# An exponential that is traced one step later: order on ScalarE in the window attention of a fused encoder layer

## The chip, the cores and the metric

The kernel runs on one core of a Trainium2 chip. The metric is the device time of one execution in microseconds, the median of several runs. TensorE is written PE, VectorE DVE, ScalarE ACT, GpSimd POOL, SyncE SP; PEld is PE's weight loading. L420 is line 420 of the kernel before.

## What is computed

One encoder layer over 1024 tokens of width 1024, all in float32. A normed input goes through one projection, whose columns feed two attentions side by side; their outputs are normed, joined and projected back; a gated MLP with a short convolution and a last norm follow. The change touches the first attention:

```python
# group A: 8 query heads, 2 key/value heads of 64, window |i-j| <= 128, blocks of 128 queries
s = einsum('bqgrd,bkgd->bgrqk', q_i, k_i) * scale          # 128 queries x up to 384 keys
s = where(valid, s, -1e30)
m = maximum(max(s, axis=-1), sink)
p = exp(s - m)
denom = sum(p, axis=-1) + exp(sink - m)                     # the sink: one more column
o = einsum('bgrqk,bkgd->bgrqd', p, v_i) / denom
```

Group B, the second attention, is a neighbourhood attention over a 16 x 64 grid of tokens with a learned bias in place of the mask and without a sink.

## The kernel before

Products in float32 precision are made from a high and a low part of each operand: ACT rounds a tile to the format that PE multiplies fast (the high part), DVE subtracts that from the original (the low part), and PE runs three products, or two where one side needs no low part.

**The units.** The first attention has 16 units (2 key heads, 8 blocks of queries). A unit has four score steps (`q_step`, one per query head) and two or three transpose steps (`t_step`, one per block of keys; 44 in all).

- A score step runs two products into a PSUM bank `s` (L393, two such banks), then calls `softmax`.
- `softmax` has POOL copy the sink column beside the scores (L415, once per pair of heads), DVE add the mask and reduce to the negated maximum `nm` (L416), ACT take the exponential in place and sum it into `sm` (L420); with the second head of a pair DVE inverts both sums (L422) and POOL scales both heads' tiles (L424).
- A transpose step has PE transpose four 128 x 128 pieces of `p` into a bank `pt` (L456, two such banks); then `split_pt` has ACT copy the high part `ph` (L430) and DVE subtract to the low part `pl` (L431).
- The value step that belongs to it runs one event later: PE multiplies `ph` (L461) and `pl` (L462) by the values into a bank `o`. Behind the last one, `leave` has ACT copy half of `o` (`ot`, L474) and DVE add the halves (`mixa`, L478).

The second attention is built the same way with its own loops: scores through the same `softmax` without a sink, transposes at L531, value products at L542 and L543.

**The order of the work.** PE's order is the order in which the program is traced, written out by hand: per unit the list "t, q, v, q, t, q, v, t, q, v" for three blocks of keys, where q is a score step of a unit two ahead. Between these events a filler traces pieces of the input projection (L179 to L181), so many per event as the table `RATES` says; the projection's other work (`evacuate` L247, weights L171 and L172, rotations L261 to L263, splits L273 and L274) comes with it. The first eight score steps are traced ahead of the first transpose step.

ACT, DVE, POOL and SP are ordered by the framework's scheduler when the program is built: it takes the instruction that is ready by its own estimate and has the lowest rank, which is its place in the trace. `tc.high_priority(offset=n)` ranks what it encloses n instructions ahead of its place, and nested offsets add up. `softmax` uses 50, `split_pt` 100, evacuations 500. `behind(name)` forces a place in the queue: what it encloses is issued behind the marked instruction if it runs on the same engine; `mark["high"]` is the last traced `ph` copy. Once built, each queue's order is fixed.

The tiles `p` hold a pair of heads; five of them rotate, with some more borrowed from another pool. `nm` and `sm` have six buffers each.

Of the kernel before, what the change touches and what calls it, by code (L numbers as in the profile page):

```python
# [15 lines left out]
AF = mybir.ActivationFunctionType  # L16
ALU = mybir.AluOpType
# [41 lines left out]
def hybrid_layer(tc, xT, w_first, w_in, w_out, w_gate, w_up, w_down, small, sink, rpb, consts, rope, out):  # L59
    nc = tc.nc  # L60
    with ExitStack() as ctx:
# [19 lines left out]
        def bank(name, tag):  # L81
            return psum.tile([128, HALF], F32, name=name, tag=tag)
# [69 lines left out]
        mark = {}  # L152

        def behind(*names):

            stack = ExitStack()
            for n in names:
                stack.enter_context(tc.issue_after(mark[n].ins))
            return stack
# [224 lines left out]
        def near(b):  # L384
            return [c for c in (b - 1, b, b + 1) if 0 <= c < NB]
# [13 lines left out]
        def pair_tile(spare=False):  # L399
# [2 lines left out]
                return lpool.tile([128, 2, 386], F32, name="p", tag="mix", bufs=slots["mix"], padded_shape=[128, 2, 512])  # L402
            return apool.tile([128, 2, 386], F32, name="p", tag="p", bufs=5, padded_shape=[128, 2, 392])

        def softmax(st, j, ps, n, bias, nsink=None):

            w = lambda ap: ap.rearrange("p (s w) -> p s w", s=2)
            p = st["p"]
            with tc.high_priority(offset=50):
                nm = spool.tile([128, 1], F32, name="nm")  # L410
                if j == 0:
                    st["sm"], st["n"] = spool.tile([128, 2], F32, name="sm"), [n, n]
                sm, st["n"][j] = st["sm"], n
                if nsink is not None and j == 0:
                    nc.gpsimd.tensor_copy(p[:, 0:2, n:n + 1], nsink.rearrange("p (j o) -> p j o", o=1))  # L415
                nc.vector.tensor_tensor_reduce(  # L416
                    out=w(p[:, j, 0:n]), in0=ps[:, 0:n].rearrange("p (w s) -> p s w", s=2), in1=bias, scale=1.0, scalar=3e38 if nsink is None else nsink[:, j:j + 1],
                    op0=ALU.add, op1=ALU.min, accum_out=nm)
                e = n if nsink is None else n + 1
                nc.scalar.activation(p[:, j, 0:e], p[:, j, 0:e], AF.Exp, bias=nm, scale=-1.0, accum_out=sm[:, j:j + 1])  # L420
                if j == 1:
                    nc.vector.reciprocal(sm, sm)  # L422
                    for i, m in enumerate(st["n"]):
                        mark["scaled"] = nc.gpsimd.tensor_scalar(p[:, i, 0:m], p[:, i, 0:m], sm[:, i:i + 1], 1.0, op0=ALU.mult, op1=ALU.mult)  # L424

        def split_pt(ps, n):
            ph = apool.tile([128, HALF], F32R, name="ph", tag="ph")
            pl = apool.tile([128, HALF], F32R, name="pl", tag="pl")
            with tc.high_priority(offset=100):
                mark["high"] = nc.scalar.activation(ph[:, 0:n], ps[:, 0:n], AF.Copy)  # L430
                mark["rest"] = nc.vector.tensor_tensor(pl[:, 0:n], ps[:, 0:n], f32(ph[:, 0:n]), op=ALU.subtract)  # L431
            return ph, pl

        def unit_window(g, b):

            cs, n = near(b), 128 * len(near(b))
            ps4 = [None] * 4
            mask = w2(cst[:, K_MA + 128 * (cs[0] - b + 1):K_MA + 128 * (cs[-1] - b + 2)])
            st = {}

            def q_step(j):
                def go():
                    if j % 2 == 0:
                        st["p"] = pair_tile(True)
                    ps, _ = scores(qa[g, j // 2][j % 2], ka[g], b)
                    softmax(st, j % 2, ps, n, mask, nsink[:, 4 * g + j - j % 2:4 * g + j - j % 2 + 2])
                    ps4[j] = st["p"][:, j % 2, :]
                return go

            def t_step(i):  # L450
                def go():
                    if i == 0:
                        st["o"] = bank("o", "o")
                    pt = bank("pt", "pt")
                    for j in range(4):
                        nc.tensor.transpose(pt[:, j * 128:(j + 1) * 128], ps4[j][:, i * 128:(i + 1) * 128], ident)  # L456
                    ph, pl = split_pt(pt, HALF)

                    def v_step():
                        o, v = st["o"], va[g]  # L460
                        nc.tensor.matmul(o, v[:, cs[i], :], mv(ph[:, :]), start=i == 0, stop=False)  # L461
                        nc.tensor.matmul(o, v[:, cs[i], :], mv(pl[:, :]), start=False, stop=i == len(cs) - 1)  # L462
                        if i == len(cs) - 1:
                            leave()
                    return v_step
                return go

            def leave():
                ot = apool.tile([128, 2, 128], F32, name="ot", tag="ot", bufs=1, padded_shape=[128, 4, 128])
                o4 = pv(st["o"][:, :])  # L470
                halved = lambda ap: ap.rearrange("p (s w) -> p s w", s=2)
                for e in range(2):
                    me, other = slice(64 * e, 64 * e + 64), slice(64 - 64 * e, 128 - 64 * e)
                    nc.scalar.activation(ot[me].rearrange("p j (s w) -> p j s w", s=2), o4[other, e::2], AF.Copy)  # L474
                    for i in range(2):
                        if mix[2 * g + i] is None:
                            mix[2 * g + i] = big("mixa", "mix")
                        nc.vector.tensor_tensor(halved(mix[2 * g + i][me, b * 128:(b + 1) * 128]), o4[me, e + 2 * i], halved(ot[me, i, :]), op=ALU.add)  # L478

            return [q_step(j) for j in range(4)], [t_step(i) for i in range(len(cs))]  # L480
# [220 lines left out]
        nsink = cpool.tile([128, 8], F32, name="nsink")  # L701
# [172 lines left out]
        order = []  # L874
# [434 lines left out]
        order = []  # L1309
# [168 lines left out]
        def finish(h, v, cols=whole, split=False):  # L1478
            n = (cols.stop - cols.start) // 128
            wide = widen(v, "pt", n)  # L1480
            again = widen(v, "pt", n) if split else wide
            copy = half("wide")
            nc.scalar.activation(copy[:, cols], again[:, 0:128 * n], AF.Copy)  # L1483
            for d in (0, 1, 3, 2, 4, 6, 5, 7):
                x = at_res(d, h, cols)
                if d in APART:
                    nc.gpsimd.tensor_tensor(x, x, copy[:, cols], op=ALU.mult)  # L1487
                else:
                    nc.vector.scalar_tensor_tensor(x, x, col(C_NFIN + d), wide[:, 0:128 * n], op0=ALU.mult, op1=ALU.mult)
                (nc.scalar if split and d in (1, 4, 5) else nc.sync).dma_start(out[d, :, h * HALF + cols.start:h * HALF + cols.stop], x)  # L1490
# [24 lines left out]
        for i, (p, j, c) in enumerate(order):  # L1515
# [4 lines left out]
            f, n = PARTS[c]  # L1520
# [146 lines left out]
```

## Time and profile before

| what | value |
|---|---|
| median of 3 runs | 1018.97 us (1018.95 to 1019.7) |
| the profiled execution's own time | 1018.9 us |
| its span | 1017.1 us |
| granted PE clock, mean | 0.997 |
| exponentials on ACT (L420), 128 of them | 75.1 us, 587 ns each |
| scalings (L424), 128 of them | 75.4 us, 601 ns each |
| high parts (L430), 108 of them | 54.8 us, 508 ns each |
| low parts (L431), 108 of them | 63.6 us, 589 ns each |

The span is the time from the first to the last instruction that the profiler recorded. The first attention's score steps start at about 53 us and its last transposes end at about 181 us; the second attention runs from there to about 346 us. Rows of the timeline read: start in us, duration in us, engine, line, operation, output and inputs, their shapes, how many in a row; in brackets the idle time of the engine before it and what ended it. Rows of a view of waits read: engine, tile and line that waited, what it waited for, then us in total, times, longest. Ends of PE's rows are modelled, so the distance from one start to the next is the better measure there.

### The profile page before, as it was taken

What the parts mean: (1) busy time and instruction counts of PE and PEld (TensorE: products, weight loads), DVE (VectorE), ACT (ScalarE), POOL (GpSimd) and SP (SyncE); (2) the same over time, 40 slices, a digit from 0 to 9 for tenths busy, and PEclk for the clock granted to TensorE, in tenths of its full rate; (3) what the DMA queues carried; (4) which work ended last, traced back from release to release, by engine and by line L of the source; (5) the groups of instructions that cost most, each with busy time, mean ns of one, the idle gap of its engine ahead of it and who ended that gap; (6) DMA issues with size and microseconds to landing.
All of it is one profiled execution on the core that took longest, in us unless ns stands there. A gap on an engine that the chain in (4) does not pass through costs nothing.

```text
span 1017.1 us, 14843 instructions
## 1 busy us (share of the span) xinstructions
PE 1006.8 (99%) x5086; PEld 889.0 (87%) x5086; DVE 833.2 (82%) x1566; ACT 561.0 (55%) x1081; POOL 103.8 (10%) x188
## 2 busy tenths in 40 slices
PE   9999999999999999999999999999999999999996
PEld 8898888999899888888888888888888888888886
DVE  7889888768888899999987786786777678996765
ACT  8567786657687554555544443444443645544451
POOL 0223333222332100000000000000000000000002
PEclk9999999999999999999999999999999999999998
DMA  8223022333234456231552333323232699966644
GB/s 294 83 73 94 30 73 65 83 83 83 84 93 136 125 193 222 82 103 64 188 191 90 111 114 114 104 94 125 93 133 85 228 329 322 312 225 235 225 153 166
DMA packets 68220, 144.94 MB, mean 142 GB/s; under 512 B 8240, under 2 KB 18736, under 8 KB 68144
## 3 DMA queue, kind: packets, MB, share of 16 engines
q1 hardware_dynamic: 58208, 118.88, 36.4%
q10 hardware_dynamic: 9936, 25.11, 6.4%
q8 instruction: 40, 0.66, 0.3%
q14 instruction: 36, 0.29, 0.1%
HBM read 103.58 MB, written 28.57 MB: 130 GB/s over the span
## 4 chain that ended last, share of the span: by engine, by line
PE 88%; DVE 6%; ACT 2%; issue 2%; DMA 1%; SPq 0%; DVEq 0%; ACTq 0%
PE x L1026 7%; PE x L1027 7%; PE x L1028 7%; PE dn L1028 7%; PE dn L1027 7%; PE dn L1026 7%; PE pj L179 7%; PE pj L181 6%; PE pj L180 6%; PE y L1027 4%; PE y L1026 4%; PE y L1028 4%; PE s L393 3%; PE z L1026 2%; PE z L1027 2%; PE z L1028 2%
## 5 line engine op out<-in xcount | busy, mean ns | idle before, releaser
L1026 PE MATMUL x<-hg,whi 128*128 128x512 f32 x352 | 133.5, 379 | 0.0
L1027 PE MATMUL x<-hg,whi 128*128 128x512 f32 x352 | 133.4, 379 | 0.0
L1028 PE MATMUL x<-hg,wlo 128*128 128x512 f32 x352 | 133.4, 379 | 0.0
L1026 PE MATMUL dn<-xd,whi 128*128 128x512 f32 (+1 forms) x330 | 120.8, 366 | 0.0
L1028 PE MATMUL dn<-xd,wlo 128*128 128x512 f32 (+1 forms) x330 | 120.6, 365 | 0.0
L1027 PE MATMUL dn<-xd,whi 128*128 128x512 f32 (+1 forms) x330 | 120.5, 365 | 0.0
L420 ACT ACTIVATE p<-p,nm 128x385 f32<-128x385 f32 (+3 forms) x128 | 75.1, 587 | 62.3 <-DVE nm L416 58.0
L1000 ACT ACTIVATE whi<-ws 128x512 fp32r<-128x512 f32 (+1 forms) x100 | 60.7, 621 | 74.2 <-DVE ws L1136 14.7
L179 PE MATMUL pj<-xgh,whi 128*128 128x512 f32 x245 | 99.7, 407 | 0.1
L424 POOL TENSOR_SCALAR p<-p,sm 128x384 f32<-128x384 f32 (+1 forms) x128 | 75.4, 601 | 196.6 <-DVE sm L422 165.8
L180 PE MATMUL pj<-xgl,whi 128*128 128x512 f32 x245 | 93.1, 380 | 0.2
L181 PE MATMUL pj<-xgh,wlo 128*128 128x512 f32 x245 | 92.9, 379 | 0.0
L1000 ACT ACTIVATE whi<-raw 128x512 fp32r<-128x512 f32 (+1 forms) x102 | 60.9, 610 | 51.0 <-PE x L1027 17.3
L1001 DVE TENSOR_TENSOR wlo<-ws,whi 128x512 fp32r<-128x512 f32 (+1 forms) x100 | 66.5, 680 | 19.2 <-ACT whi L1000 18.8
L431 DVE TENSOR_TENSOR pl<-pt,ph 128x384 fp32r<-128x384 f32 (+2 forms) x108 | 63.6, 589 | 18.1 <-ACT ph L430 16.4
L1028 PEld LDWEIGHTS x<-hg,wlo 128*128 128x128 f32 x352 | 66.5, 189 | 9.5
L1026 PEld LDWEIGHTS x<-hg,whi 128*128 128x128 f32 x352 | 66.5, 189 | 9.4
L1027 PEld LDWEIGHTS x<-hg,whi 128*128 128x128 f32 x352 | 66.5, 189 | 9.4
L1487 POOL TENSOR_TENSOR h<-h,wide 128x256 f32<-128x256 f32 (+1 forms) x6 | 5.4, 914 | 669.4 <-ACT wide L1483 669.4
L1001 DVE TENSOR_TENSOR wlo<-raw,whi 128x512 fp32r<-128x512 f32 (+1 forms) x102 | 66.5, 668 | 6.7 <-ACT whi L1000 4.5
L1028 PEld LDWEIGHTS dn<-xd,wlo 128*128 128x128 f32 x330 | 62.5, 189 | 7.9 <-DVE wlo L1001 0.3
L1027 PEld LDWEIGHTS dn<-xd,whi 128*128 128x128 f32 x330 | 62.5, 189 | 7.7
(267 smaller groups left out, 2495.0 us busy)
## 6 DMA issues: line engine op xcount, KB each, us to landing
xd<-x SPq DMA_DIRECT2D x77, 256.0 KB, 5.0
raw<-in_w_down_dram SPq DMA_DIRECT2D x72, 256.0 KB, 4.6
raw<-in_w_gate_dram SPq DMA_DIRECT2D x22, 512.0 KB, 3.5
raw<-in_w_up_dram SPq DMA_DIRECT2D x22, 512.0 KB, 3.6
x<-c ACTq DMA_DIRECT2D x22, 512.0 KB, 2.8
raw<-in_w_in_dram SPq DMA_DIRECT2D x30, 256.0 KB, 2.8
raw<-in_w_down_dram SPq DMA_DIRECT2D x36, 192.0 KB, 4.4
x<-t ACTq DMA_DIRECT2D x11, 512.0 KB, 2.6
```

What stands on the lines that cost most here:

```text
L179: nc.tensor.matmul(ps, w[0], mv(x[0][:, tsl(h)]), start=first, stop=False)
L180: nc.tensor.matmul(ps, w[0], mv(x[1][:, tsl(h)]), start=False, stop=False)
L181: nc.tensor.matmul(ps, w[1], mv(x[0][:, tsl(h)]), start=False, stop=last)
L393: nc.tensor.matmul(ps[:, 0:n], qs, k[i][:, cs[0] * 128:cs[0] * 128 + n].rearrange("p (s w) -> p w s", s=2), start=i == 0, stop=i == 1)
L420: nc.scalar.activation(p[:, j, 0:e], p[:, j, 0:e], AF.Exp, bias=nm, scale=-1.0, accum_out=sm[:, j:j + 1])
L424: mark["scaled"] = nc.gpsimd.tensor_scalar(p[:, i, 0:m], p[:, i, 0:m], sm[:, i:i + 1], 1.0, op0=ALU.mult, op1=ALU.mult)
L431: mark["rest"] = nc.vector.tensor_tensor(pl[:, 0:n], ps[:, 0:n], f32(ph[:, 0:n]), op=ALU.subtract)
L1000: nc.scalar.activation(hi, src, AF.Copy)
L1001: nc.vector.tensor_tensor(lo, src, f32(hi[:, :, :]), op=ALU.subtract)
L1026: nc.tensor.matmul(ps, w[0], x[0], start=first and i == 0, stop=False, skip_group_check=True)
L1027: nc.tensor.matmul(ps, w[0], x[1], start=False, stop=False, skip_group_check=True)
L1028: nc.tensor.matmul(ps, w[1], x[0], start=False, stop=last and i == len(ws) - 1, skip_group_check=True)
```

## The change

The exponential of a score, and with the second head of a pair the reciprocal and the two scalings, are put into a function that is kept in a list and run later. The list is emptied at three places: at the start of the next `softmax`; in a transpose step of the first attention, right behind `split_pt`, there with the exponential forced behind that step's `ph` copy on ACT; and at once, at the end of `softmax`, if there is no sink (the second attention). Wherever it is emptied, what it traces is enclosed in a priority of 50 at that place. In the second attention that place is inside `softmax`'s own block of 50.

```diff
+        deferred = []
+
+        def exponentials(*order):
+            while deferred:
+                with tc.high_priority(offset=50):
+                    deferred.pop(0)(*order)
+
         def softmax(st, j, ps, n, bias, nsink=None):
 
+            exponentials()
             w = lambda ap: ap.rearrange("p (s w) -> p s w", s=2)
...
                 e = n if nsink is None else n + 1
-                nc.scalar.activation(p[:, j, 0:e], p[:, j, 0:e], AF.Exp, bias=nm, scale=-1.0, accum_out=sm[:, j:j + 1])
-                if j == 1:
-                    nc.vector.reciprocal(sm, sm)
-                    for i, m in enumerate(st["n"]):
-                        mark["scaled"] = nc.gpsimd.tensor_scalar(p[:, i, 0:m], p[:, i, 0:m], sm[:, i:i + 1], 1.0, op0=ALU.mult, op1=ALU.mult)
+                widths = list(st["n"])
+
+                def finish(*order):
+                    with behind(*order):
+                        nc.scalar.activation(p[:, j, 0:e], p[:, j, 0:e], AF.Exp, bias=nm, scale=-1.0, accum_out=sm[:, j:j + 1])
+                    if j == 1:
+                        nc.vector.reciprocal(sm, sm)
+                        for i, m in enumerate(widths):
+                            mark["scaled"] = nc.gpsimd.tensor_scalar(p[:, i, 0:m], p[:, i, 0:m], sm[:, i:i + 1], 1.0, op0=ALU.mult, op1=ALU.mult)
+
+                deferred.append(finish)
+                if nsink is None:
+                    exponentials()
...
                     ph, pl = split_pt(pt, HALF)
+                    exponentials("high")
 
                     def v_step():
```

## The prediction

> **What bounds the kernel now.** I read the page first, for the whole span.
>
> ```profile
> span 1017.1 us, 14843 instructions
> PE 1006.8 (99%) x5086; PEld 889.0 (87%) x5086; DVE 833.2 (82%) x1566; ACT 561.0 (55%) x1081; POOL 103.8 (10%) x188
> ```
>
> PE is the bound of the program: 1006.8 of 1017.1 us. The edit removes no work from PE, so it can win only time in which PE stands still for want of something that ACT delivers. The profiled execution took 1018.9 us, 1.8 more than its span; the median shown is 1018.97. I make the sum on the span and carry it over to the median unchanged.
>
> Next I compared, in the table by windows, the stretch of the first attention in which PE isn't solid with the one behind it.
>
> ```profile
> core 0: us, PE busy (x) PEld busy (x) DVE busy (x) ACT busy (x) POOL busy (x), PEclk, DMA share, GB/s
> 65.00:110.00 45.00, 44.03 (x251) 38.64 (x249) 39.90 (x120) 33.56 (x86) 17.08 (x38) 1.00 0.30 75
> 110.00:180.00 70.00, 70.00 (x399) 62.85 (x399) 58.70 (x172) 50.07 (x128) 22.39 (x48) 1.00 0.20 55
> ```
>
> By PE's own column 45.00 - 44.03 = 0.97 us are missing between 65 and 110, and none later. By the weight loads, a clean stretch is busy 62.85 / 70.00 = 0.898 of its time, and this one 38.64 / 45.00 = 0.859: the difference is 0.039 / 0.898 x 45 = 2.0 us. The clock is 1.00 in both rows, so it explains nothing. Which of the two is the ceiling of the gain? The gaps below add up to 1.8 us, so I take 2.0.
>
> The Trainium skill (Perfetto Trace Analysis, Identifying the Most-Contended Engine) says that matmul busy time is a poor measure of TensorE's headroom and that the share of weight loads is a better one. The trace agrees: 2.0 against 0.97. By the poorer column the most that this stretch could give would be 0.97 us, 1018.0.
>
> Then the waits of the weight loads from 65 to 340 us, both attentions, and ACT's groups from 65 to 110 us (last column: idle time of ACT just before them and who ended it).
>
> ```profile
> PEld o L462 <- DVE pl L431: 2.1, 4, 0.7
> PEld o L543 <- DVE pl L431: 1.0, 2, 0.7
> PEld s L393 <- DVE nm L416: 0.4, 2, 0.2
> ```
>
> ```profile
> L420 ACT ACTIVATE p<-p,nm 128x385 f32<-128x385 f32 (+1 forms) x25 | 15.0, 598 | 10.7 <-DVE nm L416 9.0 <-POOL p L424 1.2 <-DVE sm L422 0.5
> L430 ACT ACTIVATE ph<-pt 128x512 fp32r<-128x512 f32 x18 | 10.6, 587 | 0.4 <-PE pt L456 0.2
> ```
>
> PE waits in its value products (o, L462) for the low part pl, which DVE makes from ph, which ACT makes from the transposes. ACT isn't full (33.56 of 45): it idles 9.0 us in front of exponentials whose maximum nm isn't there, and almost never (0.4) in front of ph. So ph is late not for want of ACT time, but because it stands in the queue behind an exponential that waits for DVE.
>
> **The change part by part.** Per window unit four scores are traced, one step at a time between transposes. Their exponentials (ACT), the reciprocal (DVE) and the two scalings (POOL) used to be traced with the score; now they are traced at the next score (24 of 64) or right behind the next ph (40 of 64: every one of the first 40 chunks finds exactly one pending). No instruction is added or removed: 128 exponentials, 128 scalings, no DMA, nothing on SP. What changes is order, on three queues. I replay the stalls with the durations of the rows.
>
> Stall B, the largest: ACT, then PE, then DVE.
>
> ```profile
> 98.08 0.62 ACT L420 ACTIVATE p<-p,nm 128x385 f32<-128x385 f32 x1 [0.37 <-DVE nm L416]
> 98.61 0.19 ACT L420 ACTIVATION_READ_ACCUMULATOR p<-p,nm 128x1 f32 x1
> 99.28 0.62 ACT L420 ACTIVATE p<-p,nm 128x385 f32<-128x385 f32 x1 [0.49 <-DVE sm L422]
> 100.41 0.60 ACT L430 ACTIVATE ph<-pt 128x512 fp32r<-128x512 f32 x1
> ...
> 98.06 0.60 PE L456 MATMUL pt<-cst,p 128*128 128x128 f32 x4
> 101.22 0.38 PE L461 MATMUL o<-ph,v 128*128 128x512 f32 x1
> 102.03 0.48 PE L462 MATMUL o<-pl,v 128*128 128x512 f32 x1 [0.43 <-DVE pl L431]
> ...
> 99.18 0.46 DVE L478 TENSOR_TENSOR mixa<-o,ot 64x128 f32<-64x128 f32 x2
> 100.42 0.29 DVE L478 TENSOR_TENSOR mixa<-o,ot 64x128 f32<-64x128 f32 x1 [0.78 <-ACT ot L474]
> 101.29 0.69 DVE L431 TENSOR_TENSOR pl<-pt,ph 128x512 fp32r<-128x512 f32 x1
> ```
>
> The transposes end at 98.66 and ACT is free at 98.80, but ph starts at 100.41. Behind the edit ph starts at 98.8 and ends at 99.4; the exponential of 99.28 follows it at about 99.3, because ph fills the 0.49 us in which ACT was idle. The low part fits into DVE's 0.78 us of idling before 100.42 and is done at about 100.3, before 101.22. L461 to L462 took 0.81 us where an undisturbed pair takes 0.22 (106.98 to 107.20 in the rows for POOL below); the stalled matmul's row is 0.10 longer as well (0.48 against 0.38). Worth: 0.6 + 0.1 = 0.7 us.
>
> Stall A, the same pattern: ACT, then PE.
>
> ```profile
> 88.95 0.38 ACT L474 ACTIVATE ot<-o 64x256 f32<-64x256 f32 x1
> 89.62 0.62 ACT L420 ACTIVATE p<-p,nm 128x385 f32<-128x385 f32 x1 [0.30 <-DVE nm L416]
> 90.36 0.60 ACT L430 ACTIVATE ph<-pt 128x512 fp32r<-128x512 f32 x1
> ...
> 88.02 0.60 PE L456 MATMUL pt<-cst,p 128*128 128x128 f32 x4
> 91.27 0.38 PE L461 MATMUL o<-ph,v 128*128 128x512 f32 x1
> 91.79 0.48 PE L462 MATMUL o<-pl,v 128*128 128x512 f32 x1
> ```
>
> ph can start at 89.3 instead of 90.36, a microsecond earlier; the exponential slips from 89.62 to about 89.9. Worth: 0.52 - 0.22 + 0.1 = 0.4 us.
>
> Stall C is different: ACT, DVE, PE.
>
> ```profile
> 106.84 0.59 ACT L430 ACTIVATE ph<-pt 128x512 fp32r<-128x512 f32 x1
> ...
> 107.63 0.81 DVE L172 TENSOR_TENSOR wlo<-raw,whi 128x512 fp32r<-128x512 f32 x1
> 108.76 0.68 DVE L431 TENSOR_TENSOR pl<-pt,ph 128x512 fp32r<-128x512 f32 x1
> ...
> 108.72 0.38 PE L461 MATMUL o<-ph,v 128*128 128x512 f32 x1
> 109.50 0.48 PE L462 MATMUL o<-pl,v 128*128 128x512 f32 x1 [0.40 <-DVE pl L431]
> ```
>
> Here ph is done at 107.43 and pl starts at 108.76: DVE's own queue (weights, two score additions) is what is late, and no order on ACT mends that. I leave its 0.78 - 0.22 + 0.1 = 0.7 us standing.
>
> What the move costs. The exponential comes 0.05 to 0.3 us later in A and B, and one ph (0.60) later at most; reciprocal and scalings follow it. Cover: the scaled p are wanted late. POOL, then PE:
>
> ```profile
> 102.59 1.51 POOL L424 TENSOR_SCALAR p<-p,sm 128x384 f32<-128x384 f32 x2 [1.96 <-DVE sm L422]
> ...
> 106.98 0.38 PE L461 MATMUL o<-ph,v 128*128 128x512 f32 x1
> 107.20 0.38 PE L462 MATMUL o<-pl,v 128*128 128x512 f32 x1
> 107.41 0.27 PE L456 MATMUL pt<-cst,p 128*128 128x128 f32 x1
> ```
>
> The scalings end at 104.10 and the first transpose that reads them starts at 107.41: 3.3 us of cover, the shortest of the 16 units, so I cost the delay at nothing. Were the cover gone, each of 16 units would lose up to the 0.6 us. On POOL the copy of the sink column of the next pair may fall behind a later scaling; that delays an exponential, under the same cover. On DVE the reciprocal may block the queue while its exponential is late; that happened for 0.5 us in 65 to 110 (the exponential's row above names sm for that much), and nothing that I see makes it more.
>
> The second attention changes too, though it isn't named. Its exponentials are still emitted with the score, but from inside the block of priority 50 and with another 50 around them; nested offsets add, so exponential, reciprocal and scalings now rank 100 traced instructions ahead, level with ph and pl. Where both are ready, an exponential traced before a ph now goes first. The trace of before can't show what that does. Bounds, from the stretch 275 to 337 us (who waited for ph there, then ACT, then DVE):
>
> ```profile
>   DVE pl L431: 2.7, 8
> ...
> 333.62 0.49 ACT L430 ACTIVATE ph<-pt 128x384 fp32r<-128x384 f32 x1
> 334.01 0.60 ACT L420 ACTIVATE p<-p,nm 128x384 f32<-128x384 f32 x1
> ...
> 335.05 0.54 DVE L431 TENSOR_TENSOR pl<-pt,ph 128x384 fp32r<-128x384 f32 x1
> ```
>
> At most, at the 8 chunks where DVE waits for ph, each ph falls behind one exponential of 0.6 us: 8 x 0.6 = 4.8 us slower. At best the two waits of L543 go: 1.0 us faster. I take 0, by the nearest rows: flipping the pair at 333.62 would end ph at about 334.7, still before its pl starts at 335.05, and ACT mostly issues the earlier traced exponential first already.
>
> Sum: -0.7 (B) - 0.4 (A) + 0 (C) + 0 (cover) + 0 (second attention) = -1.1 us. Span 1017.1 to 1016.0, median 1018.97 to **1017.9**. Behind 110 us PE is solid, so what is won there stays won.
>
> **The rivals.**
>
> R1, it mends more than I count. An earlier ph pulls pl forward on DVE everywhere, C dissolves too and the whole 2.0 us return, with one of the two waits of L543 (0.5): 1018.97 - 2.5 = 1016.5; with both, 1016.0. For it: DVE has 45 - 39.90 = 5.1 us idle here. Against it: in C pl stood behind ready work of DVE, not behind ACT.
>
> R2, DVE takes over. It is busy 39.90 of 45. An earlier pl (0.69) goes ahead of the score additions, nm comes later, and PE waits for the score's bank instead (L393 already waits 0.4 us, two times). The 1.1 us come back as two to four waits of 0.3: 1019.0. The Trainium skill (the same section) says to go for the engine with the highest occupancy first; here that is DVE, ahead of ACT, and by that rule an order on ACT gives nothing, 1019.0. The trace bears it out only in part, since A and B show DVE idle or on work that can wait.
>
> R3, slower: the second attention. Its exponentials, now level with ph, go ahead of it between 275 and 337 us, where PE has little reserve. With three quarters of the upper bound, 3.6 us, against the 1.1 won: 1018.97 + 2.5 = 1021.5; at the full bound 1022.7. It decides from two such chunks on (1.2 us eat the gain). For it: PE waits 1.0 us for pl there already. Against it: the replayed pair, where the flip costs nothing.
>
> That the edit doesn't do what it says is not likely: the order behind ph is forced, not left to priorities.
>
> **How the numbers follow.** A measurement of this kernel tells about 0.2%, 2.04 us, from no change: the borders are 1016.93 and 1021.01. Forecast 1017.9: 0.32, its own range 1017.0 to 1018.6, of which 0.05 lies below the lower border. R1: 0.24, of which 0.21 below it. R2: 0.12, all between. R3: 0.32, from 1019.5 upwards, of which 0.28 lies above the upper border, since a reordered queue can cost more than the rows let me price. Faster 0.26, same 0.46, slower 0.28. The range for 8 in 10 takes in R1 with both waits gone and most of R3: 1015.9 to 1022.4.
>
> **What would show it.** Right: on ACT from 65 to 110 us ph follows its transposes within about 0.5 us and the 9.0 us of waiting for nm shrink; the gaps at A and B are gone; L462's wait falls from 2.1 to about 0.7; PEld in 65 to 110 rises towards 39.9. R2: L393's wait for nm grows to 1 us or more. R3: L543's wait grows above 2 us, and exponentials precede ph there. Wrong altogether: PE waits for POOL at the transposes (L456), or ACT's idle time stands in front of ph, with PE late in return.

## The result, and the profile after

| | before | after |
|---|---|---|
| median of 11 runs each, same chip | 1018.97 us (1018.2 to 1019.97) | 1016.21 us (1015.73 to 1017.16) |
| ratio | | 0.9972, 95% interval 0.9964 to 0.998 |
| profiled execution, own time | 1018.9 us | 1016.91 us |
| its span | 1017.1 us | 1015.1 us |

The kernel is 2.76 us faster; the forecast was 1.1. The profiled execution of the changed kernel was 0.7 us slower than its median, so the two traces differ by 2.0 us only, and that much can be followed in them.

In the changed kernel the score addition is L424 (was L416), the exponential L432 (L420), the reciprocal L434 (L422), the scalings L436 (L424), the high part L446 (L430), the low part L447 (L431); in the first attention the transposes are L472 (L456) and the value products L478 and L479 (L461 and L462), in the second L548, L559 and L560 (L531, L542 and L543). Kernels of the experiments are a few lines off these.

The page of the changed kernel; the last row is that of the chain that ended last, where PE had 88% before and DVE 6%:

```profile
span 1015.1 us, 14835 instructions
PE 1006.3 (99%) x5086; PEld 890.2 (88%) x5086; DVE 832.7 (82%) x1566; ACT 561.8 (55%) x1081; POOL 104.0 (10%) x188
...
PE 99%; DVE 1%; issue 0%; ACT 0%; DVEq 0%; POOL 0%; POOLq 0%
```

PE's work is the same 1006 us; what went is time in which it stood still. The table by windows, same columns as before:

```profile
65.00:110.00 45.00, 45.00 (x261) 40.20 (x260) 41.02 (x124) 34.61 (x88) 18.10 (x40) 1.00 0.31 77
110.00:180.00 70.00, 70.00 (x399) 62.95 (x399) 58.73 (x174) 50.99 (x131) 22.44 (x48) 1.00 0.20 54
```

Between 65 and 110 us the weight loads rise from 38.64 to 40.20 of 45 us, nearly the share of the clean stretch behind it (62.95 / 70 x 45 = 40.5). The waits of the weight loads from 65 to 340 us, then ACT's groups from 65 to 110 us:

```profile
PEld o L560 <- DVE pl L447: 0.5, 2, 0.3
PEld s L393 <- DVE nm L424: 0.3, 1, 0.3
PEld o L479 <- DVE pl L447: 0.3, 1, 0.3
```

```profile
L432 ACT ACTIVATE p<-p,nm 128x385 f32<-128x385 f32 (+1 forms) x26 | 15.4, 592 | 4.4 <-DVE nm L424 4.1 <-DVE sm L434 0.3
L446 ACT ACTIVATE ph<-pt 128x512 fp32r<-128x512 f32 x18 | 10.7, 595 | 5.7 <-PE pt L472 5.5
```

The wait for the low part in the first attention falls from 2.1 to 0.3 us, that in the second from 1.0 to 0.5. ACT's idle time in front of exponentials falls from 10.7 to 4.4 us and turns up in front of the high part (0.4 to 5.7), where it means that ACT stands ready before the transposes are done.

Where the gain sits is read off the starts of five rows of PE: the first transpose, the low-part products behind A, B and C, the last such product of the first and of the second attention. In the changed kernel, leaving out what lies between:

```profile
65.21 0.27 PE L472 MATMUL pt<-cst,p 128*128 128x128 f32 x1
...
91.64 0.38 PE L479 MATMUL o<-pl,v 128*128 128x512 f32 x1
...
101.18 0.38 PE L479 MATMUL o<-pl,v 128*128 128x512 f32 x1
...
108.26 0.42 PE L479 MATMUL o<-pl,v 128*128 128x512 f32 x1
...
184.21 0.38 PE L479 MATMUL o<-pl,v 128*128 128x512 f32 x1
...
345.31 0.28 PE L560 MATMUL o<-pl,v 128*128 128x256 f32 x1
```

In the kernel before the same starts were 91.79, 102.03 and 109.50 (in the rows of A, B and C above), and

```profile
64.86 0.27 PE L456 MATMUL pt<-cst,p 128*128 128x128 f32 x1
...
185.72 0.38 PE L462 MATMUL o<-pl,v 128*128 128x512 f32 x1
...
347.20 0.28 PE L543 MATMUL o<-pl,v 128*128 128x256 f32 x1
```

The distance from one start to the next, after minus before, is -0.50 (up to A), -0.70 (A to B), -0.39 (B to C), -0.27 (C to the end of the first attention) and -0.38 us (second attention), together -2.24; the trace of after starts its transposes 0.35 us later. That shift is there at 34 us already, ahead of the first score step, so it isn't the edit's.

### The profile page after: what moved, and what is told of

Read it like the earlier page. It is cut to its first block, busy times and chain, and to the rows that moved or that the text cites. A ratio compares the mean times of both kernels' runs of the same rounds, so it can differ in the third digit from the quotient of the medians.

```text
span 1015.1 us, 14835 instructions
## 1 busy us (share of the span) xinstructions
PE 1006.3 (99%) x5086; PEld 890.2 (88%) x5086; DVE 832.7 (82%) x1566; ACT 561.8 (55%) x1081; POOL 104.0 (10%) x188
## 4 chain that ended last, share of the span: by engine, by line
PE 99%; DVE 1%; issue 0%; ACT 0%; DVEq 0%; POOL 0%; POOLq 0%
PE pj L179 8%; PE pj L181 8%; PE pj L180 8%; PE x L1045 7%; PE x L1043 7%; PE x L1044 7%; PE dn L1045 7%; PE dn L1044 7%; PE dn L1043 7%; PE s L393 4%; PE y L1045 4%; PE y L1043 4%; PE y L1044 4%; PE pt L472 2%; PE z L1043 2%; PE z L1045 2%
## 5 line engine op out<-in xcount | busy, mean ns | idle before, releaser
L432 ACT ACTIVATE p<-p,nm 128x385 f32<-128x385 f32 (+3 forms) x128 | 75.1, 587 | 47.0 <-DVE nm L424 44.1
L436 POOL TENSOR_SCALAR p<-p,sm 128x384 f32<-128x384 f32 (+1 forms) x128 | 75.6, 603 | 196.0 <-DVE sm L434 179.9
L447 DVE TENSOR_TENSOR pl<-pt,ph 128x384 fp32r<-128x384 f32 (+2 forms) x108 | 63.3, 586 | 17.4 <-ACT ph L446 16.3
L446 ACT ACTIVATE ph<-pt 128x384 fp32r<-128x384 f32 (+2 forms) x108 | 55.3, 512 | 25.8 <-PE pt L472 14.4
```

## The experiments

This table gives the same five distances for every kernel, each minus that of the kernel before, in us from one profile each, beside the ratio of the medians to the kernel before on the same chip (95% interval). One profile tells a column to about 0.2 us, at times only to 0.5: in "exponential 100" the first attention's queues are those of the kernel before, and A came out 0.46 shorter all the same; "changed kernel" and "grid as before" have the same queues there, and C differs by 0.34.

| kernel | to A | B | C | rest of first | second attention | ratio |
|---|---|---|---|---|---|---|
| changed kernel | -0.50 | -0.70 | -0.39 | -0.27 | -0.38 | 0.9972 (0.9964 to 0.998) |
| grid as before | -0.49 | -0.70 | -0.73 | -0.31 | +0.07 | 0.9983 (0.9974 to 0.9992) |
| grid only | -0.09 | +0.01 | -0.01 | +0.03 | -0.72 | 0.9992 (0.9983 to 1.0001) |
| not forced | +0.04 | -0.04 | -0.01 | +0.02 | -0.67 | 0.9998 (0.9989 to 1.0006) |
| first 27 scores | -0.49 | -0.70 | +0.04 | -0.04 | -0.58 | 0.9982 (0.9974 to 0.9991) |
| from the 28th score | -0.05 | 0.00 | 0.00 | -0.21 | -0.74 | 0.9991 (0.9982 to 1.0) |
| low part first at C | -0.09 | +0.01 | -0.42 | -0.01 | -0.08 | 0.9996 (0.9987 to 1.0005) |
| one more late | +0.57 | -0.51 | -0.20 | -0.31 | -0.49 | 0.9991 (0.9982 to 1.0) |
| all behind the high part | -0.50 | -0.70 | -0.73 | -0.31 | -0.52 | 0.9975 (0.9965 to 0.9984) |
| inverse and scale 100 | -0.10 | +0.21 | -0.01 | 0.00 | -1.00 | 0.9991 (0.9982 to 1.0) |
| exponential 100 | -0.46 | +0.01 | -0.02 | 0.00 | +0.18 | 1.0001 (0.9993 to 1.001) |
| both deferred | -0.49 | -0.70 | -0.73 | -0.31 | +0.78 | 0.9983 (0.9975 to 0.9992) |
| both findings | -0.50 | -0.70 | -0.73 | -0.31 | -0.87 | 0.9972 (0.9962 to 0.9981) |

### Which half brings what

*Grid as before*: the changed kernel, with the second attention's exponentials, reciprocals and scalings at their old rank.

```diff
                 if nsink is None:
-                    exponentials()
+                    deferred.pop()()
```

> The changed kernel, but in the second attention the exponentials, reciprocals and scalings keep their old priority of 50. Theory (the gain is the first attention's: ph no longer stands behind exponentials that wait for nm): PE is solid from 65 to 110 us as in the changed kernel, weight loads there near 40.2 us of 45, and the median is 2.0 to 2.8 us below before. In the trace the second attention falls back by at most 0.4 us, since its start differs from before only by the shift. Rival (the second attention's priority 100 brings a good part): the median is at most 1.8 us below before, and between 275 and 337 us the waits of the value products for pl return to 1.0 us of weight-load waiting.

*Grid only*: the kernel before, with the second attention's three kinds of instructions at rank 100 and nothing deferred.

```diff
+                with tc.high_priority(offset=50 if nsink is None else 0):
                     nc.scalar.activation(p[:, j, 0:e], p[:, j, 0:e], AF.Exp, bias=nm, scale=-1.0, accum_out=sm[:, j:j + 1])
                     if j == 1:
...
```

> The kernel before with the one edit that its second attention's exponentials, reciprocals and scalings rank 100 instead of 50. Theory: the first attention is untouched, 2.1 us of weight-load waiting for pl and the three gaps stay, and the median moves by less than 0.5 us, to between 1018.4 and 1019.2. Rival (that priority is worth something): 0.5 to 1.0 us faster, with L543's waits halved. The prediction's third rival (it costs): 1.2 to 4.8 us slower.

Measured: 1017.22 against 1018.96 us (-1.74) and 1018.07 against 1018.96 (-0.89). The two add up to -2.63, beside -2.76 for the whole change, and the table shows each gain in its own columns alone. So the part that the change is named for brings some two thirds, and the rank of the second attention, which it isn't named for, a third. The interval of the second one ends at 1.0001; that it is a gain rests also on the second-attention column, which is -0.4 to -1.0 in all nine kernels that raise the reciprocals' rank, and -0.08 to +0.18 in the three that leave them where they were.

### The forced place

*Not forced*: the changed kernel without the order behind the high part; the exponentials are still traced there.

```diff
-                    exponentials("high")
+                    exponentials()
```

> The changed kernel without the forced place behind ph: exponentials are traced one step later, but only their rank orders them. Theory (the forced place is what does it, since the scheduler takes nm to be ready sooner than it is and puts the exponential first again): most phs stand behind a waiting exponential as before, ACT idles 7 us or more in front of exponentials between 65 and 110 us, at least two of the three gaps are back, and the median is 0 to 1 us below before. Rival (being traced later, and so ranked behind ph, is enough): as the changed kernel, 2 us or more below before.

Measured: 1018.78, ratio 0.9998. In the weight loads from 65 to 110 us everything is back:

```profile
PEld o L479 <- DVE pl L447: 2.1, 4, 0.7
```

Tracing the exponential later is worth nothing by itself in the first attention. The place in the queue is what counts, and the scheduler, left to its ranks, puts the exponential back in front. The second attention keeps its -0.67, which the interval of the ratio takes in.

### Stall C, which I had left standing

In the changed kernel DVE's queue at C is this:

```profile
106.73 0.81 DVE L172 TENSOR_TENSOR wlo<-raw,whi 128x512 fp32r<-128x512 f32 x1
107.46 0.68 DVE L447 TENSOR_TENSOR pl<-pt,ph 128x512 fp32r<-128x512 f32 x1
108.06 0.47 DVE L424 CUSTOM_DVE_ANT_0 p<-s,cst,nsink 128x256 f32<-128x256 f32 x1
```

Before, the order was wlo, score addition, low part. The low part and the score addition have changed places. To see what it takes, I deferred one half only.

*First 27 scores* (A and B lie in this half, C doesn't), and *from the 28th score*, where the comparison is `<= 27`:

```diff
                 deferred.append(finish)
+                steps[0] += 1
                 if nsink is None:
                     exponentials()
+                elif steps[0] > 27:
+                    deferred.pop()()
```

> Only the first 27 score steps are deferred, which are those pending up to the 14th transpose step (gaps A and B); from the 28th on exponentials are traced and ranked as before. Theory of the prediction (gap C is DVE's own queue and not mended by an order on ACT near it, but it may go once DVE has caught up by what A and B win): A and B are gone; if C is gone too, it went by that catching up, and PE is solid up to 110 us. Rival (C went because the order was changed at C itself): A and B are gone and C stands with 0.4 us or more between L461 and L462 beyond the usual 0.22 us. Median 1 to 1.8 us below before if C stands, 2 or more if it is gone.

> The other half of the run before it: the first 27 score steps as in the kernel before, deferral from the 28th on (the second attention's priority stays 100). Gaps A and B must stand, 1.1 us together. If C was mended at C itself, by ph and pl of its own chunk coming earlier, C is gone here: L461 to L462 near 0.22 us, and the median 1.4 to 2.0 us below before (C 0.7, the small gaps up to 180 us 0.3, the second attention 0.7). If C was mended by DVE having caught up before it, C stands with 0.78 us and the median is 0.8 to 1.2 us below before.

Deferring around C alone does not mend it: C is 0.00, and on DVE the old order stands (score addition at 108.26, low parts from 108.66).

```profile
107.53 0.80 DVE L172 TENSOR_TENSOR wlo<-raw,whi 128x512 fp32r<-128x512 f32 x1
108.26 0.47 DVE L425 CUSTOM_DVE_ANT_0 p<-s,cst,nsink 128x256 f32<-128x256 f32 x1
...
108.66 1.28 DVE L451 TENSOR_TENSOR pl<-pt,ph 128x512 fp32r<-128x512 f32 x2
```

Deferring the first 27 alone mends A and B, and the gap of the low part at C goes too, but the score in front of it is late instead:

```profile
103.08 0.38 PE L181 MATMUL pj<-xgh,wlo 128*128 128x512 f32 x1
103.97 0.38 PE L393 MATMUL s<-ka,q 128*128 128x256 f32 x1 [0.51 <-DVE nm L425]
```

From 103.08 to 103.97 are 0.89 us where an undisturbed matmul takes 0.22: 0.67 us, and C's column is +0.04. That is the sign that rival R2 was to show, at one place, but not by its mechanism: the low part stands ahead of this score addition in the kernel before too. Here DVE stood idle for ACT three times just before (0.24, 0.17 and 0.16 us), and a split wlo took 0.95 us. At C itself DVE has another order again, with wlo behind the low part (107.29 and 108.42). With both halves deferred C's gap goes, and 0.3 us of the score's is left in the profile of the changed kernel, none in "grid as before". That leaves DVE's order as the suspect; the next kernel makes the exchange of the changed kernel by hand.

*Low part first at C*: the kernel before, one score addition forced behind the low part on DVE.

```diff
+                count[0] += nsink is not None
+                with behind(*["rest"] * (nsink is not None and count[0] == 32)):
                     nc.vector.tensor_tensor_reduce(
...
```

> The kernel before with nothing deferred and one single forced order on DVE: the 32nd score addition of the first attention goes behind the last traced low part. On DVE near 108.5 us this puts the low part ahead of that score addition; ACT's queue changes in one place behind it only. Theory (stall C is DVE's queue order alone, and what mended it in the changed kernel is this exchange): the wait at C shrinks from 0.56 to 0.1 to 0.2 us, A (0.3) and B (0.6) stand, PE is 0.4 us ahead of before behind C; if the score behind it is then late, a new wait for the score bank of 0.3 to 0.7 us stands within 3 us of C and the gain is gone. Rival (C needs an earlier high part from ACT): C keeps its 0.5 us. The total is 0 to 0.5 us below before, about what the measurement can tell.

```profile
107.30 0.80 DVE L172 TENSOR_TENSOR wlo<-raw,whi 128x512 fp32r<-128x512 f32 x1
108.03 0.68 DVE L435 TENSOR_TENSOR pl<-pt,ph 128x512 fp32r<-128x512 f32 x1
108.63 0.47 DVE L420 CUSTOM_DVE_ANT_0 p<-s,cst,nsink 128x256 f32<-128x256 f32 x1
...
108.39 0.38 PE L465 MATMUL o<-ph,v 128*128 128x512 f32 x1
108.76 0.48 PE L466 MATMUL o<-pl,v 128*128 128x512 f32 x1
```

PE went from the one product (108.39) to the other (108.76) in 0.37 us in place of 0.78, and the column of C alone moves, by -0.42; no new wait for a score bank follows. Up to C this exchange is the only one on the engines' queues. So C is a matter of DVE's order, as the prediction read it. What the prediction missed is that DVE's order is itself worked out when the kernel is built, and an edit of ACT's order elsewhere changes it. That the low part is placed ahead because it is ready earlier by the scheduler's estimate is likely, but no run shows it.

### How late an exponential may be

*One more late*: one exponential always stays pending, so each comes about one score later still.

```diff
-        def exponentials(*order):
-            while deferred:
+        def exponentials(*order, keep=0):
+            while len(deferred) > keep:
...
-            exponentials()
+            exponentials(keep=1)
...
-                    exponentials("high")
+                    exponentials("high", keep=1)
```

> The changed kernel with every deferred exponential held back one step more (one stays in the list whenever it is emptied). It tests the cover that the prediction counted on: the scalings end 3.3 us or more ahead of the first transposes that read them in the kernel before, 1.8 to 4.6 us in the changed one. One step more is 1 to 1.5 us on PE. Theory (the cover is real and is not yet used up): the shortest covers shrink to 0.5 to 1.5 us, PE does not wait for POOL, and the median is that of the changed kernel within 0.4 us. Rival (the delay is not free): PE waits for POOL at the transposes in several units and the median is 0.5 to 4 us above the changed kernel.

Measured: 1018.32 against 1019.16, ratio 0.9991; about 1.9 us of the 2.76 are gone. It is not the cover of the scaled tiles: no wait of PE for POOL is in this trace. POOL, then PE, at the unit where the cover is shortest:

```profile
99.45 1.15 POOL L436 TENSOR_SCALAR p<-p,sm 128x384 f32<-128x384 f32 x2 [4.40 <-DVE sm L434]
...
100.43 0.38 PE L479 MATMUL o<-pl,v 128*128 128x512 f32 x1
100.65 0.60 PE L472 MATMUL pt<-cst,p 128*128 128x128 f32 x4
```

The scalings end at 100.60 and the transposes start at 100.65, right behind the product before them: nothing lost, with 0.05 us of cover left. In the changed kernel the shortest cover is 1.80 us, at the second unit:

```profile
67.95 1.31 POOL L436 TENSOR_SCALAR p<-p,sm 128x384 f32<-128x384 f32 x2 [2.34 <-DVE sm L434]
...
71.06 0.38 PE L472 MATMUL pt<-cst,p 128*128 128x128 f32 x2
```

What came back is ACT's queue:

```profile
L432 ACT ACTIVATE p<-p,nm 128x385 f32<-128x385 f32 (+1 forms) x26 | 15.4, 594 | 10.2 <-DVE nm L424 8.0 <-DVE sm L434 2.3
```

ACT idles 8.0 us for maxima again, and between 65 and 110 us the weight loads wait 1.5 us for low parts and 0.6 for a maximum. Which exchange puts the exponentials with a missing maximum in front again was not taken apart.

*All behind the high part*: from the first transpose step on, the exponentials of the first attention are emitted there only, not also at the next score.

```diff
-            exponentials()
+            if "high" not in mark:
+                exponentials()
             w = lambda ap: ap.rearrange("p (s w) -> p s w", s=2)
```

> The changed kernel, but in the first attention an exponential is emitted only behind a ph, not at the next score step: the 24 that are emitted at a score now queue behind the next ph as well. Theory (every exponential that waits for nm ahead of a ph is a risk): ACT's idle time in front of exponentials between 65 and 110 us falls from 4.1 us to under 2.5, no gap over 0.1 us is left there, and the median is 0 to 0.4 us below the changed kernel. Rival (two exponentials in a row behind one ph come too late for the scaled p, or hold up the next ph): 0.3 us or more above it.

```profile
L433 ACT ACTIVATE p<-p,nm 128x385 f32<-128x385 f32 (+1 forms) x25 | 14.7, 591 | 0.1
L447 ACT ACTIVATE ph<-pt 128x512 fp32r<-128x512 f32 x19 | 11.3, 595 | 9.3 <-PE pt L473 9.1
```

```profile
65.00:110.00 45.00, 45.00 (x263) 40.66 (x262) 42.27 (x128) 34.31 (x89) 18.65 (x40) 1.00 0.30 77
```

Here the idle time before exponentials is gone to 0.1 us, the stretch is clean (40.66 of 45) and C is worth its full 0.73. In the profile of the changed kernel a wait for a score bank stood at 103.1 us (0.3 us); "grid as before", with the same queues there, has the 0.73 too, so this part isn't shown to be the edit's. The ratio, 0.9975, can't be told from the changed kernel's 0.9972.

### What the second attention gives, and by which instruction

*Inverse and scale 100* and *exponential 100*: the kernel before, with one part of "grid only" each.

```diff
                 nc.scalar.activation(p[:, j, 0:e], p[:, j, 0:e], AF.Exp, bias=nm, scale=-1.0, accum_out=sm[:, j:j + 1])
-                if j == 1:
+                with tc.high_priority(offset=50 if nsink is None else 0):
+                    if j == 1:
...
```

> The kernel before with one thing changed: in the second attention the reciprocal (DVE) and the scalings (POOL) rank 100 instead of 50; the exponentials stay. On DVE the reciprocal then stands ahead of the low part in five places. Theory (what the second attention gives comes from the reciprocal going first, which starts POOL's scalings 0.3 to 0.4 us earlier and takes them off DVE's splits of two SBUF tiles): the 0.48 us wait at about 333 us shrinks to about 0.15, and the total is 0.5 to 0.9 us below the kernel before. Rival (it is the exponentials' place on ACT and the score additions that follow from it): the wait at 333 us stays and the total is within 0.2 us of before.

```diff
-                nc.scalar.activation(p[:, j, 0:e], p[:, j, 0:e], AF.Exp, bias=nm, scale=-1.0, accum_out=sm[:, j:j + 1])
+                with tc.high_priority(offset=50 if nsink is None else 0):
+                    nc.scalar.activation(p[:, j, 0:e], p[:, j, 0:e], AF.Exp, bias=nm, scale=-1.0, accum_out=sm[:, j:j + 1])
```

> The counterpart: only the exponentials of the second attention rank 100; reciprocal and scalings stay at 50. Theory (reciprocal first): the 0.48 us wait at about 333 us stays, total within 0.3 us of before. Rival (exponentials): the total is 0.5 to 0.9 us below before and the wait at 333 us shrinks. The third theory of the prediction, exponentials level with the high parts go ahead of them and PE waits for it: 1 us or more above before.

Measured: 1018.04 against 1018.93 with the reciprocals (-0.89, column -1.00), 1019.15 against 1018.93 with the exponentials (+0.2, column +0.18). All of the gain is the reciprocals': in "inverse and scale 100" the queues of ACT and POOL are those of the kernel before, and DVE's differs in five places only, where a reciprocal stands ahead of a low part. One of them is just ahead of the wait at 335 us. The kernel before, DVE, POOL and PE:

```profile
332.58 0.41 DVE L431 TENSOR_TENSOR pl<-pt,ph 128x256 fp32r<-128x256 f32 x1
332.91 0.15 DVE L422 RECIPROCAL sm<-sm 128x2 f32<-128x2 f32 x1
...
333.45 0.93 DVE L172 TENSOR_TENSOR wlo<-raw,whi 128x512 fp32r<-128x512 f32 x1
334.30 0.82 DVE L559 TENSOR_TENSOR mixb<-o,ot 64x512 f32<-64x512 f32 x1
...
333.25 1.57 POOL L424 TENSOR_SCALAR p<-p,sm 128x384 f32<-128x384 f32 x2 [4.71 <-DVE sm L422]
...
335.00 0.33 PE L542 MATMUL o<-ph,v 128*128 128x384 f32 x1
335.64 0.43 PE L543 MATMUL o<-pl,v 128*128 128x384 f32 x1 [0.32 <-DVE pl L431]
```

"Inverse and scale 100", the same place:

```profile
332.04 0.15 DVE L423 RECIPROCAL sm<-sm 128x2 f32<-128x2 f32 x1
332.11 0.39 DVE L432 TENSOR_TENSOR pl<-pt,ph 128x256 fp32r<-128x256 f32 x1
...
332.91 0.68 DVE L172 TENSOR_TENSOR wlo<-raw,whi 128x512 fp32r<-128x512 f32 x1
333.51 0.67 DVE L560 TENSOR_TENSOR mixb<-o,ot 64x512 f32<-64x512 f32 x1
334.11 0.54 DVE L432 TENSOR_TENSOR pl<-pt,ph 128x384 fp32r<-128x384 f32 x1
...
332.35 1.70 POOL L425 TENSOR_SCALAR p<-p,sm 128x384 f32<-128x384 f32 x2 [4.25 <-PE pt L532]
...
334.75 0.33 PE L543 MATMUL o<-ph,v 128*128 128x384 f32 x1
334.91 0.33 PE L544 MATMUL o<-pl,v 128*128 128x384 f32 x1
```

The reciprocal goes 0.3 us ahead within DVE's queue, so POOL's scalings start ahead of the weights' split instead of almost level with it. From the start of wlo to the start of the next low part DVE then takes 334.11 - 332.91 = 1.20 us instead of 335.05 - 333.45 = 1.60. PE goes from one product to the other in 0.16 us instead of 0.64, so it lost 0.48 us here, of the column's 1.00; about 0.2 more lie at 276 us, the rest in steps too small to place. The 0.40 us of DVE are most of that; the rest is that wlo starts 1.84 us ahead of PE's first product instead of 1.55. 0.25 of the 0.40 are wlo's, beside POOL's scalings; the rest is mixb's, whose records in the trace of before have a median of 0.79 us with and without a scaling beside them, so POOL does not explain that part. The exponentials' rank is rival R3's mechanism: on ACT three of them go ahead of a high part. Over the whole kernel its cost can't be told from nothing (0.9993 to 1.001), and 0.2 us is far from the 0.6 us for each that R3 was priced with. In the trace of "exponential 100" it shows at this same place: PE takes 0.95 us from one product to the other (334.26 to 335.21) instead of 0.64. The high part is done in time there (at 334.05), but DVE has put a score addition (334.27) ahead of the low part (334.61).

### Deferring the second attention too

*Both deferred*: the second attention's exponentials go behind its own high parts as well, or to the next score, so with its reciprocals and scalings they are back at rank 50, at a later place.

```diff
                 deferred.append(finish)
-                if nsink is None:
-                    exponentials()
...
                     ph, pl = split_pt(pt, 128 * len(bs))
+                    exponentials("high")
```

> The changed kernel with the same deferral in the second attention too (exponential behind the next ph or at the next score, priority 50). Theory (the same pattern costs there: ph waits 1 to 2 us after its transposes between 275 and 337 us): ph follows its transposes within 0.6 us there, the gaps at 274 and 333 us go, and the median is 0.2 to 0.8 us below the changed kernel. Rival (there DVE is what is late, and the scaled p have less cover): no faster than the changed kernel, with PE waiting for POOL at L548's transposes or for nm at the scores.

```profile
PEld pj L180 <- DVE mgl L633: 1.1, 1, 1.1
PEld pj L179 <- PE s L393: 1.1, 1, 1.1
```

The waits for the low part there are gone, and two others of 1.1 us stand in their place: one product of the projection waits for the low part of its operand (mgl, DVE), another, into a bank `pj`, by PE's own rows for a subtraction on DVE (v, L335, 0.8 us). The column is +0.78, and the whole is 1017.29 against 1019.16, 1.87 us below before where the changed kernel is 2.76. The recipe does not carry over to the second attention, where the filler's own operands are made by the same DVE queue; which instruction of the new order delays mgl was not taken apart.

### The version that the runs point to

*Both findings*: "all behind the high part" with the second attention's reciprocals and scalings at 100 and its exponentials at 50.

```diff
                         nc.scalar.activation(p[:, j, 0:e], p[:, j, 0:e], AF.Exp, bias=nm, scale=-1.0, accum_out=sm[:, j:j + 1])
-                    if j == 1:
+                    with tc.high_priority(offset=50 if nsink is None else 0):
+                      if j == 1:
...
                 if nsink is None:
-                    exponentials()
+                    deferred.pop()()
```

> The version that the runs point to: in the first attention every exponential behind the high part alone, as in the run that emits them only there; in the second attention the reciprocal and the scalings rank 100 and the exponentials stay at 50. Against the run with all behind the high part it differs in three exchanges on ACT and two on DVE. Theory (the exponentials' rank 100 costs about 0.2 us, the reciprocal's gives 1.0): PE is 2.6 to 2.8 us ahead of before at the end of the second attention, instead of 2.5, ratio 0.997, which the measurement can't tell from the changed kernel's 0.9972. Rival (the exchanges matter together, with the earlier high parts of the first attention gone by then): no gain over 2.5, or a loss of 0.3 us.

Measured: 1016.12 against 1019.05, ratio 0.9972 (0.9962 to 0.9981). In its profile no weight load waits for a low part or a maximum from 65 to 340 us, and the columns add up to -3.11 against the changed kernel's -2.24. In the medians, 1016.12 and 1016.21, the two can't be told apart.

## Why the prediction was right in sign and short in size

- **What bounds the kernel, and the ceiling** held. PE's own column would have allowed 0.97 us between 65 and 110; the weight loads said 2.0. A, B and C alone gave 0.50 + 0.70 + 0.73 = 1.93 us in "all behind the high part".
- **Stalls A and B** held in mechanism and size: -0.4 and -0.7 forecast, -0.49 to -0.50 and -0.70 in all six kernels that defer the early scores by one score behind a forced place.
- **Stall C is the first step that failed**: "no order on ACT mends that. I leave its 0.78 - 0.22 + 0.1 = 0.7 us standing." Half of it was right, for the delay was DVE's queue ("low part first at C": -0.42 by one exchange on DVE), and an order on ACT near C alone left it as it was ("from the 28th score": 0.00). But with the whole first attention deferred DVE's queue is ordered differently, and C gives 0.39 to 0.73 us. The step took DVE's order from the trace of before as if it were given; it is an output of the same scheduler that the edit feeds. Rival R1 had C dissolve, and was argued away with that reason.
- **The cover of the scaled tiles** held at a cost of nothing: 1.80 us were left at the shortest, and even 0.05 us, in "one more late", cost PE nothing there.
- **The second attention is the second step that failed**: "I take 0, by the nearest rows". It measured -0.89 us by itself. The step said that exponential, reciprocal and scalings now rank 100 and then priced the exponential only, by flipping one pair on ACT. The exponentials' cost can't be told from nothing (+0.2 us); the reciprocals brought 0.9 to 1.0. The replayed pair also took DVE's order as given: as replayed, the exchange on ACT left the high part early enough, but with it a score addition went ahead of the low part, and PE lost 0.3 us more there. The lower bound of the term, 1.0 us faster, was where the time lay.
- **The rest of the first attention** gave another 0.3 us behind C in the kernels that defer all of it, where the prediction counted nothing because PE's column showed no gap behind 110 us. By the weight loads, 62.85 to 62.95, a little was there to win.
- **R1's number** is where the time came out: 1016.21 lies below the forecast's own 1017.0 to 1018.6, between R1's 1016.5 and 1016.0. Its mechanism is right in half: C did dissolve, but the waits of the second attention shrank by the reciprocals' rank and not by earlier high parts, for in "grid as before" 0.9 of their 1.0 us are left.
- **R2** did not come: the wait for a score bank was 0.4 us in all before and is 0.3 in the changed kernel. It grows to 1.1 us in "first 27 scores" and 0.6 in "one more late", so it is a risk of such edits. The Trainium skill (Perfetto Trace Analysis, Identifying the Most-Contended Engine) says to optimize the engine with the highest occupancy first. DVE was busy 39.90 of 45 us and ACT 33.56, so that would have put DVE ahead of this change. The prediction read it as saying that an order on ACT gives nothing, which the page doesn't say, and the runs show otherwise: "grid as before", whose edit is an order on ACT's queue, gained 1.74 us, for ACT was late at an occupancy of 0.75 because of what stood at the head of its queue. Orders on DVE were worth something too: 0.42 us at C, and 0.89 with the reciprocals.
- **The sum**, with the terms as they were measured: 0.49 + 0.70 + 0.73 + 0.31 from "grid as before" and 0.72 from "grid only" are 2.95 us, against 2.76 measured (0.9964 to 0.998 of 1018.97 is 2.0 to 3.7 us). The changed kernel's own profile shows 2.24, less at C and in the second attention. The interval takes in both sums, so no further cause is needed, though one of a few tenths of a microsecond isn't ruled out.

## What to carry to other kernels

An instruction that waits on another engine holds up ready work behind it in its queue, even on an engine that is a quarter idle: look at what an engine's idle time stands in front of, and move the waiting instruction behind the ready one by a forced place, since in the first attention ranks alone changed nothing. When an edit changes when data is ready, a scheduler that orders all queues at build time gives other queues a new order too, so compare the built queues of all engines before counting a stall as untouched. When a priority is raised around several instructions, price each of them by its own queue: here the cheapest, a reciprocal of 0.15 us, carried the gain.

## What the runs showed of the hardware

A split of two SBUF tiles on DVE (wlo, 128x512) took 0.68 us in "inverse and scale 100" and 0.93 in the kernel before, with the same operands; in the second case POOL had started its scalings 0.2 us earlier. Where wlo started just as POOL came to its second scaling (332.35 plus one scaling of some 0.55 us, 332.9), wlo kept its 0.68 and POOL's pair took 1.70 us. An undisturbed pair of the changed kernel:

```profile
334.54 1.04 POOL L436 TENSOR_SCALAR p<-p,sm 128x384 f32<-128x384 f32 x2 [1.82 <-DVE sm L434]
```

So the two stand in each other's way. In the kernel before, wlo came second and paid 0.25 us, and POOL's pair took 1.57 us, so both paid; in "inverse and scale 100" POOL alone did. Over the whole trace of before, by whether a record of a scaling overlaps: the splits of weights (wlo) have a median of 0.684 us without (127 records) and 0.861 us with one (15 records). Low parts of the same size (pl, first attention), which read one input from PSUM, have 0.69 us either way.

The Trainium skill (SBUF — State Buffer, Who interferes with whom) says that DVE and GpSimd share a pair of ports under an exclusive lock, that a DVE instruction with two SBUF inputs contends with a GpSimd instruction that reads SBUF, and that one with at most one SBUF input, outside the two-port modes, does not. For the first kind its Summary: rules for kernel authors adds that the second one to issue is blocked in full until the first finishes. The rows agree in direction and in who pays: wlo has two SBUF inputs, the low parts have one. In size, a full block would have held wlo of the kernel before to the end of POOL's first scaling, about 333.8 (333.25 plus the same 0.55), and then for 0.68 us, to 334.5; its record ends at 333.45 + 0.93 = 334.38. With spans on POOL as rough as they are, that comes close, and doesn't settle it.
